# Softmax with temperature on one core: the first tile's store cut in two, its first half on Pool's queue behind the first pass

## The chip, the cores and the metric

The kernel runs on one core of a Trainium2 chip; the other cores are idle. The metric is the device time of one execution in microseconds, as the median of several runs; lower is better.

## The reference

```python
def reference(x, temperature):          # x: 32 x 512 x 1024 float32, temperature 0.5
    scaled = x / temperature
    shifted = scaled - np.max(scaled, axis=-1, keepdims=True)
    exp_x = np.exp(shifted)
    return (exp_x / np.sum(exp_x, axis=-1, keepdims=True)).astype(np.float32)
```

These are 16,384 rows of 1,024 numbers: 67.11 MB to read and as much to write.

## The kernel before

The rows are cut into 16 tiles of 128 partitions with eight rows each (4.19 MB). A tile is loaded by SyncE's queue, Vector takes the maxima, Scalar the exponentials and their sums, Vector divides in place, and Scalar's queue stores the tile from the same buffer. Six buffers are shared by all tiles. The first and last two tiles are computed in two passes of four rows, all others in one pass of eight. A tile is stored as a whole in both cases, after its last pass:

```python
ROWS = 8
BUFS = 6
PASSES = [[4, 4]] * 2 + [[8]] * 12 + [[4, 4]] * 2
...
    def store(g):
        i, a, k = groups[g]                 # tile, first row of this pass, its rows
        if a + k == ROWS:
            nc.scalar.dma_start(out=dram(of, i), in_=tiles[i])
            load()                          # the next tile, into a buffer that comes free
...
        for _ in range(BUFS):
            load()
        for g in range(len(groups) + 1):
            ...
            if g < len(groups):
                maximum(g)
                exponential(g)
            if g > 0 and not alone:
                divide(g - 1)
                store(g - 1)
```

## Time and profile before

| What | Value |
|---|---|
| Time, median of the first 3 runs | 317.11 us (317.06 to 317.88) |
| Span of the profiled run | 316.0 us |
| Vector busy | 251.0 us, 79% |
| Scalar busy | 148.1 us, 47% |
| Load queue and store queue, share of the 16 DMA engines | 49.8% and 49.2% |
| Mean rate | 425 GB/s |

Busy shares alone would point at Vector. But the last two shares in the table are of the same 16 engines and have to be added.

### The profile page before, as it was taken

How to read it: one execution, taken by the hardware profiler on the slowest of the kernel's cores; microseconds unless marked ns; L12 is line 12 of the kernel's file. 1: busy time of each engine (PE TensorE's matmuls, PEld its weight loads, DVE VectorE, ACT ScalarE, POOL GpSimd, SP SyncE). 2: the span in 40 equal slices, each digit the busy share in tenths (PEclk: the TensorE clock that was granted, in tenths of full speed). 3: DMA queues.
4: the chain of work that ended last, by engine and by line, in shares of the span. 5: the costliest groups of instructions: out<-in, count | busy, mean ns of one | idle time of the engine just before them, and what ended most of it. 6: DMA issues, size and time to landing. Idle time of an engine off the chain costs nothing. (4 is left out here: it accounts for less than half of the span.)

```text
span 316.0 us, 530 instructions
## 1 busy us (share of the span) xinstructions
DVE 251.0 (79%) x146; ACT 148.1 (47%) x257; POOL 0.2 (0%) x4
## 2 busy tenths in 40 slices
DVE  0399999999689794997939979299793999979710
ACT  0176637680907428083380924708247091564700
POOL 0000000000000000000000000000000000000000
DMA  8999999999999999999999999999999999999996
GB/s 328 415 448 423 377 456 407 460 403 456 408 452 415 452 402 444 419 452 411 452 415 452 427 436 432 431 436 427 436 427 448 415 448 419 448 415 456 407 456 282
DMA packets 4611, 134.24 MB, mean 425 GB/s; under 512 B 512, under 2 KB 512, under 8 KB 512
## 3 DMA queue, kind: packets, MB, share of 16 engines
q1 hardware_dynamic: 2304, 67.11, 49.8%
q10 hardware_dynamic: 2304, 67.11, 49.2%
q14 instruction: 3, 0.02, 0.0%
HBM read 67.11 MB, written 67.11 MB: 425 GB/s over the span
## 5 line engine op out<-in xcount | busy, mean ns | idle before, releaser
L77 ACT ACTIVATE xt<-xt,bias 128x1024 f32<-128x1024 f32 x128 | 145.1, 1135 | 136.7 <-DVE bias L71 127.2
L68 DVE TENSOR_REDUCE top<-xt 128x8 f32<-128x8192 f32 (+1 forms) x20 | 139.5, 6976 | 44.6 <-DMA xt<-in_x_dram 44.6
L95 DVE TENSOR_SCALAR xt<-xt,recip 128x1024 f32<-128x1024 f32 x80 | 54.3, 749 | 0.5
L92 DVE TENSOR_TENSOR xt<-xt,recip 128x8192 f32<-128x8192 f32 x6 | 52.2, 8692 | 0.2
L77 ACT ACTIVATION_READ_ACCUMULATOR xt<-xt,bias 128x1 f32 x128 | 23.8, 186 | 0.0
L77 ACT ACT_TABLE_LOAD x1 | 1.3, 1283 | 13.3 <-DMA xt<-in_x_dram 13.3
L89 DVE RECIPROCAL recip<-sums 128x8 f32<-128x8 f32 (+1 forms) x20 | 3.7, 187 | 4.1 <-ACT xt L77 4.1
L71 DVE TENSOR_SCALAR bias<-top 128x8 f32<-128x8 f32 (+1 forms) x20 | 3.4, 170 | 0.7
L138 POOL MEMSET const-bfloat16-1.0<- 128x1 bf16 x1 | 0.1, 101 | 0.0
L138 POOL MEMSET const-uint8-127<- 128x1 uint8 x1 | 0.1, 101 | 0.0
L138 POOL MEMSET const-float32-0.0<- 128x1 f32 x1 | 0.1, 98 | 0.2 <-issue 0.2
L138 POOL MEMSET const-float32-1.0<- 128x1 f32 x1 | 0.1, 98 | 0.0
## 6 DMA issues: line engine op xcount, KB each, us to landing
xt<-in_x_dram SPq DMA_DIRECT2D x16, 4096.0 KB, 49.7
out_dram<-xt ACTq DMA_DIRECT2D x16, 4096.0 KB, 29.5
```

Of the source, the lines that this page charges most:

```text
L68: nc.vector.tensor_reduce(out=top, in_=tiles[i][:, a : a + k, :], axis=mybir.AxisListType.X, op=extreme)
L71: nc.vector.tensor_scalar_mul(bias, in0=top, scalar1=-scale)
L77: nc.scalar.activation(tiles[i][:, a + b, :], tiles[i][:, a + b, :], mybir.ActivationFunctionType.Exp, bias=bias[:, b : b + 1], scale=scal ...
L89: nc.vector.reciprocal(recip, sums)
L92: nc.vector.tensor_mul(xt, xt, recip.unsqueeze(2).to_broadcast([P, k, d]))
L95: nc.vector.tensor_scalar_mul(tiles[i][:, a + b, :], in0=tiles[i][:, a + b, :], scalar1=recip[:, b : b + 1])
L138: nc = _bacc.Bacc("TRN2", target_bir_lowering=False, num_devices=1)
```

## The change

The intent is to let stores begin earlier. The first four rows of the first tile are ready at 25.55 us, and the store of the whole tile is issued at 32.98. Now the first half goes out by Pool's queue, idle otherwise, as soon as the first pass is divided; the second half goes by Scalar's queue at the old place. All other tiles are stored as before.

```diff
     def store(g):
         i, a, k = groups[g]
+        if i > 0:
+
+            a, k = 0, a + k
+        if i == 0 or k == ROWS:
+
+            queue = nc.gpsimd if g == 0 else nc.scalar
+            queue.dma_start(out=dram(of, i)[:, a : a + k, :], in_=tiles[i][:, a : a + k, :])
         if a + k == ROWS:
-            nc.scalar.dma_start(out=dram(of, i), in_=tiles[i])
             load()
```

## The prediction

> **What bounds the kernel now.** I read the page first (busy slices, queues), then the busy time by stages, then the timeline of the first 60 us and the landing times of single transfers, last the chain that ended last.
>
> The page of the kernel before:
>
> ```profile
> DVE 251.0 (79%) x146; ACT 148.1 (47%) x257; POOL 0.2 (0%) x4
> ...
> DMA  8999999999999999999999999999999999999996
> ...
> q1 hardware_dynamic: 2304, 67.11, 49.8%
> q10 hardware_dynamic: 2304, 67.11, 49.2%
> ```
>
> Vector has 65 us to spare, Scalar more. The 16 DMA engines are at 9 or more tenths in every slice but the first and the last; the load queue (q1) takes 49.8% of their span, the store queue (q10) 49.2%, together 99.0%. So the DMA engines are the bound, and no slice between has room. The packets tell their size: 67.11 MB in 2304 packets over 16 transfers is 144 a transfer, of which 16 are small completion packets and 128 carry 32 KB each, one partition's eight rows.
>
> Busy time by stages of the kernel before (the last two columns are DMA share and GB/s):
>
> ```profile
> 2.10:10.00 7.90, 0.00 (x0) 0.00 (x0) 0.00 (x0) 1.00 0.95 402
> 10.00:20.00 10.00, 6.69 (x3) 3.35 (x4) 0.00 (x0) 1.00 1.00 433
> 20.00:33.00 13.00, 12.68 (x15) 9.97 (x19) 0.00 (x0) 1.00 1.00 434
> 33.00:37.00 4.00, 4.00 (x1) 1.76 (x4) 0.00 (x0) 1.00 0.99 344
> 37.00:40.00 3.00, 2.93 (x7) 2.49 (x5) 0.00 (x0) 1.00 1.00 404
> ...
> 52.00:84.00 32.00, 31.81 (x15) 21.09 (x37) 0.00 (x0) 1.00 1.01 436
> 84.00:240.00 156.00, 128.03 (x60) 74.31 (x131) 0.00 (x0) 1.00 1.00 432
> 240.00:281.00 41.00, 35.15 (x22) 20.60 (x37) 0.00 (x0) 1.00 1.00 432
> ```
>
> Loads alone (10 to 33 us) run at 433 to 434 GB/s, loads and stores together (52 to 281) at 432 to 436. So it does not matter to the total when stores start: bytes cost the same alone or mixed. The one dip is 33 to 40 us, when the first store is issued: the engines are counted busy at 99% yet move 344 and then 404 GB/s.
>
> Account of the span: 134.24 MB at 432 GB/s is 310.7 us. The first load is issued at 0.73 and lands 12.5 us later, where 4.19 MB at 432 needs 9.7, so the start costs 0.73 + 2.8 = 3.5. The dip costs 4 x (432 - 344)/432 + 3 x (432 - 404)/432 = 0.8 + 0.2 = 1.0. The last store is issued at 301.13 and lands 14.0 us later, at 315.1, which leaves 0.9 to the end. 310.7 + 3.5 + 1.0 + 0.9 = 316.1, against a span of 316.0. Of all this, only the dip of 1.0 us is anything that a different first store could touch.
>
> The timeline around the first store:
>
> ```profile
> 22.81 2.74 DVE L95 TENSOR_SCALAR xt<-xt,recip 128x1024 f32<-128x1024 f32 x4
> ...
> 25.47 4.42 DVE L68 TENSOR_REDUCE top<-xt 128x4 f32<-128x4096 f32 x1
> ...
> 30.20 2.74 DVE L95 TENSOR_SCALAR xt<-xt,recip 128x1024 f32<-128x1024 f32 x4
> ...
> 32.98 0.37 ACTq L102 DMA_DIRECT2D out_dram<-xt  x1
> ...
> 52.02 0.34 ACTq L102 DMA_DIRECT2D out_dram<-xt  x1
> ```
>
> The first four rows are divided by 25.55 and lie there until 32.98. The second tile's store comes only at 52.02.
>
> **What the Trainium skill says.** "DMA: Bandwidth & Descriptors", section "Issuing engines are not separate DMA queues": DMAs from any engine run on the same 16 engines and interleave, and issuing from several saves only issue time. The trace agrees: two queues together move 432 GB/s, one alone 434. The same page, "Queues, rings and completion order": each engine serves its queues in turn, packet by packet. The trace agrees over the run (49.8% against 49.2%); a 4 MB store beside loads takes about twice 9.7 us. "SBUF — State Buffer", section "Who interferes with whom": Pool's software-made descriptors can be held up while Vector runs a two-port operation such as tensor_scalar, never by tensor_reduce. No DMA of Pool is in this trace, so it is not shown here; but Vector runs a 4.42 us reduce exactly when the first half is ready, so I expect no hold-up. "DMA: Bandwidth & Descriptors", "Latency and other measured facts", puts the first byte at about 1 us for Pool's path and 0.6 us for the other; the trace shows longer waits: the first load lost 2.8 us, and the store of 32.98 moved nothing on its queue until after 37 (from 33 to 37 only q1 shows).
>
> **The change part by part.** The order of instructions on Vector, SP and PE is the same as before. Scalar's first store becomes 128x4096 in place of 128x8192; Pool gets one 128x4096 store, waiting for Vector and the first load. Every other store is the same single transfer.
>
> - Added: one issue on Pool, idle otherwise (0.2 us busy): nothing on a path. One more set of 16 completion packets, tiny beside 4608. The tile's 128 packets of 32 KB become 256 of 16 KB; at 2 MB each half is still large. I estimate 0 to 0.3 us for both.
> - Moved: 2.1 MB of stores, 4.85 us of DMA time at 432, begins at about 27 to 30 (25.55 plus 1 to 4.4 us) in place of 37.4. In turn with loads it takes 9.7 us and ends at 37 to 40. The loads fall up to 4.85 us behind at that point.
> - Given back: the second half (issued at 32.98 as before) runs from about 37 to 40 until 47 to 50. Then the store queue is empty until the second tile's store, issued at 52.02, a time that Vector sets (18.86 us busy of 19.0 from 33 to 52). Its first packets come between 53.4 and 56.4, taking the 1.4 to 4.4 us of above. Meanwhile loads run alone at full rate and regain what they lost. In the kernel before, the first store lands at 32.98 + 24.7 = 57.7. So from about 57 on, both kernels have moved the same, within 2 us of store work.
> - Released earlier: the seventh load waits for the first tile's stores and can be issued at about 49 in place of 57.7. It gains nothing: the sixth load, issued in the first microseconds, lands up to 85.0 us after its issue, so the load queue has work until some 87 us and the seventh is queued 29 us too early already.
> - The onset dip: it may move with the first store (no change), be paid again when the Scalar queue starts or restarts after its empty time (+1.0 each), or be smaller with half a store. I take half of one more dip, +0.5.
>
> On the path: 0 to 0.3 for packets, +0.5 for the dip, 0 for the rest; minus 0.1 for a chance that the dip gets smaller. Sum +0.4 to +0.6; I take +0.4. 317.11 + 0.4 = 317.5.
>
> **The end.** Does a shift early reach the end? The last load is issued at 232.79 and lands 49.8 us later, at 282.6; Vector takes up its tile at 284.24, 1.6 us later, because the tile before is divided first. The chain of waits runs through that tile's exponentials and divisions to the store at 301.13. The store before it is issued at 284.36 and lands 21.2 us later, at 305.6, so the last store is 4.4 us early for the DMA engines, of which a queue start might need some. Together 1.6 + up to 4.4 us of slack. If stores are ahead by 0.2 to 2 us, the last load comes up to twice that later, since it shares the engines to its end, thus 0.4 to 4. That fits inside the slack, nearly whole.
>
> **Rivals.** First, the earlier store is a gain, since the mix starts 10 us sooner and the buffer is free sooner. For it: seven microseconds in which a finished half waits. Against: no empty DMA time there (434 GB/s with loads alone), and a ready load waits 29 us anyway. It could win the dip at most: 316.1 to 316.6. Second, a new cost: Pool's path moves its packets slower or unevenly over the 16 engines, and the queue that stops and restarts pays the dip twice more. For it: the dip of 1.0 is real and falls on the onset of a store queue; every engine is full, so what one loses is never regained. Against: only 2.1 of 134 MB goes this way. It makes 318.5 to 319.5. Third, the tail becomes the bound: loads end so late that the last tile's compute is exposed. It needs stores more than 2 to 3 us ahead; it makes 318 to 320. Fourth, Pool's descriptors are held up past 30.2 by Vector's divisions: then both halves go out at about 33 as before, and the time is 317.1.
>
> **Range and chances.** The runs before spread from 317.06 to 317.88. Down I can see 1.0 us at most, up about 2. So 316.6 to 319.0 for 8 in 10. Two per cent is 6.3 us, more than the whole account outside the bytes holds (5.4): a gain of that size is next to impossible, a loss needs something that no view shows. Chances 0.01, 0.97, 0.02.
>
> **What would show it.** Right: mean DMA rate within 2 of 425 GB/s, 9s in every slice between, a new store queue of 2.1 MB beginning before 31 us, the seventh load issued near 49 us and yet no earlier arrival downstream, the second tile's store at 52.0, the last load's landing within 4 us of 282.6. A dip below 400 GB/s near 27 to 31 or 53 to 56 us shows the added onset. Wrong: an empty stretch in the load queue, Vector waiting for the last tile past 286 us, a slow last slice, or a longer time ahead of the first load because Pool's queue has to be made ready.

## The result

The changed kernel takes 317.33 us (median of 6 runs, 317.24 to 318.28), the kernel before 317.26 us (median of 6, 317.06 to 318.08). The ratio is 1.0002, with a 95% interval of 0.9985 to 1.0019: the same. A ratio here is the mean time of one kernel's fast runs over that of the other's of the same rounds, so it is not quite the ratio of the medians.

The page of the changed kernel; the columns of the queue lines are packets, MB and share of the 16 engines:

```profile
DVE 251.1 (80%) x146; ACT 148.1 (47%) x257; POOL 0.9 (0%) x5
...
DMA  8999999999999999999999999999999999999996
...
q1 hardware_dynamic: 2304, 67.11, 49.8%
q10 hardware_dynamic: 2304, 65.01, 47.7%
q0 software_dynamic: 144, 2.10, 1.6%
```

The busy row of the DMA engines has the same digits as before. The store queue's 49.2% has become 47.7 + 1.6 = 49.3%: work has moved from one queue to another, and none has gone.

Busy time by stages of the changed kernel; the last two columns are DMA share and GB/s:

```profile
25.00:28.00 3.00, 3.00 (x2) 1.81 (x4) 0.66 (x1) 1.00 0.95 404
28.00:31.00 3.00, 2.93 (x5) 1.17 (x3) 0.00 (x0) 1.00 0.98 377
31.00:34.00 3.00, 3.00 (x4) 3.00 (x6) 0.00 (x0) 1.00 0.97 350
34.00:37.00 3.00, 2.98 (x1) 0.47 (x2) 0.00 (x0) 1.00 1.03 442
37.00:40.00 3.00, 2.95 (x7) 2.78 (x5) 0.00 (x0) 1.00 1.00 431
...
84.00:240.00 156.00, 129.03 (x62) 74.66 (x133) 0.00 (x0) 1.00 1.00 433
240.00:281.00 41.00, 35.16 (x22) 20.57 (x37) 0.00 (x0) 1.00 1.01 435
```

The dip has moved with the first store. Before, it lay at 33 to 40 us; now the rate is low from 25 to 34 and back at 431 to 442 where the dip used to be. Its size, against 432: 3 x (28 + 55 + 82 - 10)/432 = 1.1 us, as before within what such windows resolve (in the kernel before, 3 us windows between 25 and 34 us, ahead of the dip, range from 415 to 448). The packet records of the traces measure it without window edges. A 32 KB load packet takes 1.213 us; in the 8 us after the issue of the first store some take up to 2.3 us. All time over 1.213, divided by 16 engines, is 0.95 us in the kernel before and 0.84 us here after Pool's issue. After Scalar's issues at 32.69 and 51.73 it is 0.00, so there was no second dip. In the kernel before, 21 of the 29 slow packets start ahead of the store's own first packet (37.02).

The timeline around the first stores of the changed kernel (start, duration, engine, line, operation; idle time before it in brackets):

```profile
25.18 4.41 DVE L68 TENSOR_REDUCE top<-xt 128x4 f32<-128x4096 f32 x1
...
25.57 0.66 POOL L107 DMA_DIRECT2D out_dram<-xt  x1 [25.12 <-DVE xt L95]
...
32.69 0.37 ACTq L107 DMA_DIRECT2D out_dram<-xt  x1
...
51.73 0.34 ACTq L107 DMA_DIRECT2D out_dram<-xt  x1
...
52.95 8.69 DVE L68 TENSOR_REDUCE top<-xt 128x8 f32<-128x8192 f32 x1 [1.26 <-DMA xt<-in_x_dram]
...
53.76 0.33 SPq L59 DMA_DIRECT2D xt<-in_x_dram  x1
```

Pool's issue took 0.66 us beside Vector's reduce, which kept its 4.41 us. The price stands in the line of 52.95. The store took DMA time from the loads, so the fourth tile's load came late and Vector waited 1.26 us for it. In the kernel before, it took up the same tile without a pause:

```profile
51.90 8.68 DVE L68 TENSOR_REDUCE top<-xt 128x8 f32<-128x8192 f32 x1
```

The issues of the changed kernel, with the KB of each and the time from issue to landing:

```profile
out_dram<-xt POOLq DMA_DIRECT2D x1, 2048.0 KB, 22.7
out_dram<-xt ACTq DMA_DIRECT2D x1, 2048.0 KB, 21.0
```

The first half lands at 25.57 + 22.7 = 48.3 and the second at 32.69 + 21.0 = 53.7. The whole store of before landed at 57.7. The tile's buffer is thus free 4.0 us sooner, and the seventh load is issued at 53.76. While both halves are in flight, three queues take turns: from 38 to 46 us the loads moved 61 packets in 57.8% of the engines' time, the first half 54 in 24.8% and the second 51 in 24.3%.

At the end little is left of this. The last load lands at 283.3 (issued at 231.09, 52.2 us to landing), before at 282.6. The last store is issued at 301.87, before at 301.13, and it lands after 12.8 us, at 314.7, where it was 315.1 before. Vector's 0.7 us of delay went into slack.

### The profile page after: what moved, and what is told of

It is laid out like the page before. It is cut to its first block, busy times and chain, and to the rows that moved or that the text cites. A ratio compares the mean times of both kernels' runs of the same rounds, so it can differ in the third digit from the quotient of the medians.

```text
span 315.5 us, 534 instructions
## 1 busy us (share of the span) xinstructions
DVE 251.1 (80%) x146; ACT 148.1 (47%) x257; POOL 0.9 (0%) x5
## 3 DMA queue, kind: packets, MB, share of 16 engines
q1 hardware_dynamic: 2304, 67.11, 49.8%
q10 hardware_dynamic: 2304, 65.01, 47.7%
## 5 line engine op out<-in xcount | busy, mean ns | idle before, releaser
L107 POOL DMA_DIRECT2D out_dram<-xt x1 | 0.7, 655 | 25.1 <-DVE xt L95 25.1
## 6 DMA issues: line engine op xcount, KB each, us to landing
out_dram<-xt POOLq DMA_DIRECT2D x1, 2048.0 KB, 22.7
```

The source lines that it names most:

```text
L107: queue.dma_start(out=dram(of, i)[:, a : a + k, :], in_=tiles[i][:, a : a + k, :])
```

## The experiments

All kernels were run beside the kernel before on the same chip.

**e1: both halves on Scalar's queue.** Pool's path is taken away and the early half kept.

```diff
-            queue = nc.gpsimd if g == 0 else nc.scalar
+            queue = nc.scalar
```

> Both halves of the first tile by Scalar's queue, nothing on Pool. Theory A (the DMA engines are full from the first load to the last store, so the place and the queue of the first store cost and win nothing): 317.3 us, within 0.5 of before and after. Rival B (the early start wins about 1 us and Pool's path costs about 1 us, and the two cancel): without Pool's path the win alone is left, 316.3 us. It also settles the share of the first half beside the loads: if the engines take turns by time, the half (4.85 us of work) lands about 14 us after its issue; if by packets, with 16 KB packets against the loads' 32 KB, it has a third of the time and lands 18 to 20 us after.

Measured: 317.24 us against 317.19, ratio 1.0001 (0.9984 to 1.0018). There is no gain without Pool, so no gain is hidden behind a cost of Pool's path; rival B, which expected 316.3, is out by nearly 1 us. The first half's issue in e1, and the queues' packets, MB and share of the engines from 32 to 44 us:

```profile
out_dram<-xt ACTq DMA_DIRECT2D x1, 2048.0 KB, 20.1
...
q1 hardware_dynamic: 118, 3.34, 66.2%
q10 hardware_dynamic: 112, 1.67, 32.5%
```

The turns are by packet: both queues moved nearly as many packets, but a packet of the store has 16 KB and one of the loads 32, so the half gets a third of the time. Three times 4.85 is 14.6 us; most of the rest of the 20.1 is the wait for its first packet, which starts at 29.3, 4.0 us after the issue. In even time it would have landed after some 14 us.

This run also shows the slack of the end: its last store was issued at 298.14, 3.7 us earlier than in the changed kernel, and landed after 16.7 us, at 314.8, hence not earlier.

**e2: the opposite of the change.** The first tile's store is held back to the second tile's.

```diff
-        if a + k == ROWS:
+        if a + k == ROWS and i > 0:
+            if i == 1:
+                nc.scalar.dma_start(out=dram(of, 0), in_=tiles[0])
+                load()
             nc.scalar.dma_start(out=dram(of, i), in_=tiles[i])
             load()
```

> The opposite of the change: the first tile's store is held back by some 19 us and issued together with the second tile's, at about 52 us. Theory A: the six loads keep the engines full until about 60 us, so nothing is lost, 317.3 within 0.6; the dip of about 1 us moves to 52 to 57 us. Rival B (early mixing is worth about 1 us for 7 us): 2 to 3 us slower, 319 to 320.

Measured: 317.22 us against 317.19, ratio 1.0004 (0.9989 to 1.0018). The first store is issued at 51.50 in place of 32.98, with no effect on the time. The dip goes along: the stage from 33 to 37 us runs at 418 GB/s in place of 344, and the load packets after 51.50 lose 0.67 us. Between the changed kernel (25.57) and this one lie 26 us of first-store time, and the time doesn't depend on it. While loads are queued, the engines don't need stores.

**e3: one store left out.** Its output is wrong, which doesn't matter for the time.

```diff
-            nc.scalar.dma_start(out=dram(of, i), in_=tiles[i])
+            if i != 8:
+                nc.scalar.dma_start(out=dram(of, i), in_=tiles[i])
```

> Wrong on purpose: the store of tile 8 (4.19 MB) is left out, all compute and all loads stay. Theory A: 4.19 MB at 432 GB/s less, 9.7 us, so 307.6 within 0.7. Rival C (the compute of the tail or the waits for buffers set the end, and DMA time in the middle is partly hidden): less than half of it, 312 to 317.

Measured in a single run: 307.47 us, 9.7 us less than 317.19. That is the DMA time of the bytes left out (4.19 MB at 432 GB/s).

**e4: a fifth of Vector's work left out.** Its output is wrong, which doesn't matter for the time.

```diff
         nc.vector.reciprocal(recip, sums)
+        if 4 <= i < 12:
+            return
```

> Wrong on purpose: the divisions of tiles 4 to 11 are left out, about 56 us of Vector's 251 (four whole-tile ones of 8.7 us and four times eight rows, 5.4 us), all DMAs stay. Theory A: no change, 317.3 within 0.7, and stores are issued up to 9 us earlier in the middle. Rival C (Vector's pace still sets part of the time): faster by 2 us or more, 315 or less.

Measured in a single run: 317.22 us against 317.19. Its page, below, has Vector at 62% in place of 79%. Here 56 us of the busiest compute engine are worth nothing, while e3 shows 9.7 us of DMA work worth 9.7.

```profile
DVE 194.6 (62%) x110; ACT 148.0 (47%) x257; POOL 0.2 (0%) x4
```

**e5: all stores on Pool's queue.** The suspected cost is taken 32 times.

```diff
-            nc.scalar.dma_start(out=dram(of, i), in_=tiles[i])
+            nc.gpsimd.dma_start(out=dram(of, i), in_=tiles[i])
```

> The suspected cost of Pool's path taken 32 times: all 16 stores go by Pool's queue, whole tiles as before. Theory A: its packets take the same 1.21 us as Scalar's queue's, 317.3 within 1. Rival B (Pool's path costs about 1 us on 2.1 MB): at least several us slower, 320 to 330. A hold-up of Pool's descriptors by Vector's divisions would show as stores that start several us later after their issue than the 4 us seen so far.

Measured: 317.57 us against 317.21, ratio 1.0010 (0.9995 to 1.0025). The median is 0.36 us up, with an interval that holds 1. Shared among 32 portions of 2.1 MB that is 0.01 us each: for the change, nothing. The issues took 531 to 1013 ns, and the stores landed after 14.2, 29.1 and 33.0 us (shortest, median, longest), against 14.0, 29.5 and 33.4 in the kernel before. The 1013 ns are the one issue that met Vector's divisions; the others took 531 to 667:

```profile
260.83 1.01 POOL L102 DMA_DIRECT2D out_dram<-xt  x1 [22.37 <-ACT xt L77]
260.97 5.39 DVE L95 TENSOR_SCALAR xt<-xt,recip 128x1024 f32<-128x1024 f32 x8
```

That is a hold-up of about half a microsecond, in one case, and this store landed after 24.5 us, as the same store of the kernel before did.

**e6: all stores in halves.** The smaller packets are taken 16 times.

```diff
-            nc.scalar.dma_start(out=dram(of, i), in_=tiles[i])
+            for h in (0, 4):
+                nc.scalar.dma_start(
+                    out=dram(of, i)[:, h : h + 4, :], in_=tiles[i][:, h : h + 4, :]
+                )
```

> The other cost of the change, smaller packets, taken 16 times: every store is two of four rows, both on Scalar's queue at the place of the whole one. Theory A: a 16 KB packet takes 0.611 us where half of 1.213 is 0.607, 0.7% of 155 us of stores, 1.1 us, and 256 more completion packets: 317.5 to 319. In turns by packet the stores get a third while loads are queued, so they land later (about 30 us after issue rather than 24 for the first) and loads run ahead early, which must not change the total. Rival: smaller packets cost nothing that can be seen, 317.3.

Measured: 328.13 us (326.19 to 329.71) against 317.21, ratio 1.0339 (1.0297 to 1.0382). The expectation failed by a factor of about ten. The end of this run by stages:

```profile
304.00:312.00 8.00, 1.77 (x3) 0.00 (x0) 0.00 (x0) 1.00 1.00 428
312.00:316.00 4.00, 0.00 (x0) 0.00 (x0) 0.00 (x0) 1.00 0.89 381
316.00:320.00 4.00, 0.00 (x0) 0.00 (x0) 0.00 (x0) 1.00 0.19 82
320.00:326.00 6.00, 0.00 (x0) 0.00 (x0) 0.00 (x0) 1.00 0.05 22
```

By the packet records fifteen engines are done by 319 us, most of them by 317. A share of 0.05 to 0.06 is one engine of 16, and that one goes on alone to 325. The turns are again by packet: from 38 to 60 us the loads moved 208 packets in 66.2% of the engines' time and the stores 212 in 34.1%. Later, Scalar waited 93.2 us for loads, seven times, where in the kernel before only its wait at the start (13.3) was for a load; but Vector's waits for loads fell from 44.6 to 32.1 us, so these waits alone explain nothing. e9 and e10 look for the cause.

**e7: the first tile's store held back to 84 us.**

```diff
+        if a + k == ROWS and i > 0:
+            nc.scalar.dma_start(out=dram(of, i), in_=tiles[i])
+            if i == 3:
+                nc.scalar.dma_start(out=dram(of, 0), in_=tiles[0])
+                for _ in range(4):
+                    load()
+            if i > 3:
+                load()
-        if a + k == ROWS:
-            nc.scalar.dma_start(out=dram(of, i), in_=tiles[i])
-            load()
```

> Theory A has a limit that this looks for: the first tile's store is held back until after the fourth tile's, about 84 us, and the seventh load, which needs that buffer, with it. Up to then there are six loads (58 us) and two stores (19 us) to move, 77 us of work from 2 us on, so the engines must run empty for about 4 us before 84 and perhaps again while only stores are queued. Expected 321 to 326, with a slice between 70 and 90 us under 9 tenths. If it is still 317.3, the engines' time is not what sets the end and theory A falls.

Measured: 319.16 us against 317.21, ratio 1.0059 (1.0044 to 1.0074). The expectation was too high, and its premise was wrong: the seventh load was issued at 72.26, before the first tile's store at 84.10, so it had been given another buffer, by its time that of the second tile, whose store landed at 72.2 (51.77 + 20.4). The empty stretch expected did not come. What was lost stands here:

```profile
74.00:80.00 6.00, 5.93 (x6) 1.80 (x3) 0.00 (x0) 1.00 0.97 355
80.00:92.00 12.00, 12.00 (x7) 7.36 (x14) 0.00 (x0) 1.00 1.01 413
92.00:240.00 148.00, 125.06 (x61) 73.31 (x128) 0.00 (x0) 1.00 1.00 433
```

Against 432 this is 6 x 77/432 + 12 x 19/432 = 1.6 us of the 2.0 lost, in the stretch where the load queue had run out (from 70 to 76 us only the store queue shows) and set in again. The packet records show the dip three times here, after the issues at 51.77 (0.59 us), 72.26 (0.91) and 84.10 (0.59), where the kernel before has it once. Here, then, is the limit of "it doesn't matter": moving stores costs once the load queue runs out.

**e8: a tiny store ahead of everything.** Is the dip a cost of the first store of any size?

```diff
+        seed = stats.tile([P, 1], f32, name="seed")
+        nc.gpsimd.memset(seed, 0.0)
+        nc.scalar.dma_start(out=dram(of, 0)[:, 0, 0:1], in_=seed)
         for _ in range(BUFS):
             load()
```

> What the dip is: a store of one number per partition (512 bytes in all, overwritten later by the first tile's store) is issued by Scalar's queue ahead of everything, at about 1 us. If the dip of 0.9 us is a one-time cost of the first store of any size, it moves to the first microseconds, and the stage from 33 to 40 us runs at 425 GB/s or more; the total is 316.4 if it is then hidden by the start, 317.3 if not. If the dip belongs to the first large store, it stays where it was at 33 to 40 us, 344 to 404 GB/s.

Measured: 317.35 us against 317.21, ratio 1.0002 (0.9986 to 1.0019). The dip stays at the first large store:

```profile
33.00:37.00 4.00, 4.00 (x1) 1.62 (x4) 0.00 (x0) 1.00 0.97 328
37.00:40.00 3.00, 2.93 (x7) 2.62 (x5) 0.00 (x0) 1.00 1.14 492
```

The 492 of the second line is above the steady rate and gives back part of the first, so the two windows alone leave only 0.5 us; in the packet records the loss is 0.86 us against 0.95. It is not a one-time cost of the queue's first use. What it is stays open. It comes at the first large store whatever its queue (e5, on Pool's: 0.77 us). The changed kernel pays it once, although two queues begin; e7 shows it where loads set in again.

**e9: loads and stores all in halves.** To e6's edit, this is added:

```diff
-            nc.sync.dma_start(out=xt, in_=dram(xf, i))
+            for h in (0, 4):
+                nc.sync.dma_start(out=xt[:, h : h + 4, :], in_=dram(xf, i)[:, h : h + 4, :])
```

> All stores halved cost 11 us, ten times what was expected; this tells two causes apart. Here loads and stores both go in two halves of four rows (16 KB packets on both queues), so the two queues are again in even turns. If the loss came from uneven turns (stores a third of the time, loads two thirds, so that loads run ahead, their queue empties and restarts again and again, and one DMA engine is left behind at the end): 317 to 318.5, no load queue that runs empty, a last slice as in the kernel before. If small packets or the number of transfers as such are slow: 326 or more.

Measured: 319.08 us against 317.16, ratio 1.0060 (1.0044 to 1.0077). This is a little above the range expected (317 to 318.5). The packets are as small as in e6 and twice as many, yet more than four fifths of the 11 us are gone. So small packets as such were a fifth of it at most. The 1.9 us that are left are near what the packet records give: 0.611 us for 16 KB, twice of which is 0.7% more than 1.213 for 32 KB, and 0.7% of 310.7 us is 2.2.

**e10: only the loads in halves.** The loads are cut as in e9, and the stores are whole.

> The uneven turns the other way round: loads in halves (16 KB packets), stores whole (32 KB). While both are queued the stores have two thirds of the time, so a store is done sooner than the next is computed, the store queue empties and waits for compute instead of the load queue for buffers. If any unevenness costs, 320 or more; if only loads that run dry against the buffers cost, 317 to 318.5.

Measured: 329.96 us (328.88 to 332.09) against 317.16, ratio 1.0412 (1.0372 to 1.0453). Uneven turns cost in this direction too, but through another door. The end of e10 by stages, and the last chain in its timeline:

```profile
304.00:312.00 8.00, 6.83 (x7) 3.87 (x7) 0.00 (x0) 1.00 0.48 205
312.00:316.00 4.00, 2.92 (x5) 0.77 (x2) 0.00 (x0) 1.00 0.00 0
316.00:320.00 4.00, 0.00 (x0) 0.00 (x0) 0.00 (x0) 1.00 0.92 393
```

```profile
303.42 4.42 DVE L69 TENSOR_REDUCE top<-xt 128x4 f32<-128x4096 f32 x1 [10.56 <-DMA xt<-in_x_dram]
...
315.78 0.34 ACTq L103 DMA_DIRECT2D out_dram<-xt  x1
```

With more than half of the time going to stores (57.6% from 38 to 60 us), the loads fall behind. Vector waits 10.56 us for the end of the last load, and then the engines run empty for some 8 us (8 x 0.52 + 4) while the last tile is computed. This is the prediction's third rival, the tail as the bound, and it needs an unevenness that lasts.

For e6 the cause is narrowed and not settled. Uneven turns are shown to be needed: the loss comes with either side halved alone and nearly goes with both (e9). The queue shares split it. In the kernel before the engines are busy for 99.0% of 316.0 us, 312.8 us; in e6 for 97.0% of 326.1, 316.3 us; in e10 for 96.9% of 327.7, 317.5 us. So 3.5 us of e6's loss and 4.7 of e10's are more packet time, and the rest is engines standing still. Why one of 16 engines ends some 6 us after the others in e6 is open.

## Why the prediction was right

**The bound.** Right. The DMA engines set the time: e3 (9.7 us of bytes, 9.7 us of time) and e4 (56 us of Vector, nothing) show it, and e2 shows that mixing early or late is the same. The rate in the middle hardly changed, 433 to 435 GB/s against 432. One reading on the way was loose: the first load's first packet starts at 1.73 us, 1.0 us after its issue, so the 2.8 us that this load lost are not a wait for the first byte alone, as the prediction has it.

**Added: packets and Pool's issue, 0 to 0.3 us.** Right as far as can be measured. e5 puts Pool's path at 0.01 us for such a portion, and 0.7% on 4.19 MB is under 0.1 us. One more set of 16 small packets was right: the page counts 528 under 512 B, before 512; that they signal completion is not shown by the traces. What was not seen is that packet size sets the turns; if all transfers of one side are cut, that costs 3 to 4% (e6, e10).

**The onset dip, half of one more, +0.5 us.** Too high. The dip moved with the first store and was paid once, 1.1 us against 1.0 by windows and 0.84 against 0.95 by packets. The prediction's sign of an added onset, under 400 GB/s near 27 to 31 us, did come (377), but the old dip was gone, which the sign had not asked for. This term is why a loss of 0.4 us was predicted. Measured is 0.07 (317.33 against 317.26), and the interval, about -0.5 to +0.6 us, can't tell the two apart. That 317.5 lies so near to 317.33 is partly luck: the kernel before, taken as 317.11, later measured 317.26. The sum has a slip, too: 0 to 0.3, plus 0.5, minus 0.1 is 0.4 to 0.7, not 0.6.

**Moved and given back.** Right in kind, wrong in size. The first half was to end at 37 to 40 us and the second at 47 to 50; they landed at 48.3 and 53.7. The step "in turn with loads it takes 9.7 us" failed, because turns go by packet and not by time (e1: 20.1 us to landing; with the third queue beside it, 22.7 in the changed kernel). What the prediction gave as the trace's agreement, 49.8% against 49.2% over the run, could not show this: both queues move the same bytes in the same packets, so the shares come out even in any order. The end of the exchange, near 57 us, still came as described: from 52 us on stores and loads ran at the old rate, with loads later by 0.7 us at the end.

**Released earlier.** The seventh load was issued at 53.76 rather than 49, for the same reason, and it gained nothing, as told. That the loads regain in time what they lost failed slightly: Vector waited 1.26 us for the fourth tile's load.

**The end.** Right: last load at 283.3 (282.6 plus at most 4 was foreseen), last store 0.74 us later, landing no later. e1 measured the slack directly: 3.7 us earlier, landing the same.

**Rivals.** The gain by an early start is excluded by e1 and e2; a cost of Pool's path by e5; the tail as the bound didn't occur in the changed kernel, but e10 shows that it exists. Pool's hold-up didn't occur: its issue lay beside a reduce and took 0.66 us. In e5 one issue met a division and took 1.01 us, without a later landing.

## What to carry to other kernels

Where the DMA engines are full from end to end, add the shares of the queues first: if they come near 100%, moving a transfer earlier only takes time from another one, as long as both queues stay supplied (e7 shows where that ends), and only bytes or idle engine time are worth work. In this kernel it also paid to keep the contiguous runs of competing transfers equal in size: a store queue with runs half as long got a third of the engines' time (e6), and halving one side alone cost 3 to 4%, while halving both cost 0.6%.

## What the Trainium skill lacked or had wrong

- "DMA: Bandwidth & Descriptors", section "Queues, rings and completion order", says that engines take turns by packet. It lacks the consequence: a queue with 16 KB packets, as the profile counts them, beside one with 32 KB gets a third of the time (34.1% against 66.2% in e6 from 38 to 60 us). The two kernels in which one side is halved throughout lose 10.9 us (e6) and 12.8 us (e10) of 317.
- The same page's "Rules for kernel authors" gives 128 partitions and at least 1 MiB per DMA for the highest bandwidth. e6 and e10 keep both and lose 3.4% and 4.1%; with sizes that match on the two queues (e9) the loss is 0.6%.
- The same page's "Latency and other measured facts" gives 0.6 us to the first byte for this kind of queue. On idle engines the first load's first packet came 1.0 us after its issue (0.73 to 1.73). Beside queued loads the first store of the kernel before, issued at 32.98, moved nothing until 37: over 4 us.
- No page has the dip: at the first large store loads slow down, 344 and 404 GB/s in place of 432 over 7 us; load packets take up to 2.3 us in place of 1.213, and 0.7 to 0.95 us are lost (before, after, e1, e2, e5, e8). It moves with the store (e2; e8 excludes first use of the queue); its cause is open.
- "SBUF — State Buffer", section "Who interferes with whom", agrees as far as it was tried: Vector's reduce kept its 4.41 us beside Pool's issue of 0.66 us, and the one issue of e5 that met a tensor_scalar took 1.01 us in place of 0.53.
